# A hybrid encoder layer on one core: the rest of the modulation moved to column quarters of TensorE, with an earlier load of each head's decays and a longer pause in the DeltaNet inverse

## The chip, the core and the metric

The kernel runs on one core of one Trainium2 chip. The metric is the device time of one execution in microseconds (us), the median of several runs. All data is float32; the large products are done as three products of a split into a rounded part and a rest (float32r), so that they keep float32's precision.

The engines are named as in the profile: PE is TensorE (its weight loads are PEld), DVE is VectorE, ACT is ScalarE, POOL is GpSimd, SP is SyncE, whose queue issues nearly all transfers. Each engine, SP's queue too, works through its own instructions in order: one that waits holds up all that stand behind it.

## What is computed

One layer for 512 prompt frames and 64 sample frames, width 2048. A vector `c` for each of the two streams gives six modulation vectors; they scale and shift the input of the mixer and of the feed-forward part, and gate both results.

```python
mod = jax.nn.silu(c) @ w_ada[l] + b_ada[l]
sh1, sc1, g1, sh2, sc2, g2 = jnp.split(mod[:, None, :], N_MOD, axis=-1)
h = rmsnorm(x, norm1[l]) * (1 + sc1) + sh1
mix, s_a, s_b, s_c = token_mixers(h, ...)        # 4 GLA heads and 8 DeltaNet heads
x = x + g1 * mix
h = rmsnorm(x, norm2[l]) * (1 + sc2) + sh2
f, s_f = conv_ffn(h, ...)
x = x + g2 * f
```

`w_ada` is 2048 x 12288. The DeltaNet recurrence of a head needs, for each block of frames, decays `exp(G_i - G_j)`, a triangular inverse and products with it:

```python
decay = jnp.exp(jnp.where(causal, big_g[..., :, None] - big_g[..., None, :], -jnp.inf))
lower = jnp.where(strict, jnp.einsum('bhid,bhjd->bhij', kb, k) * decay, 0.0)
sol = lax.linalg.triangular_solve(eye + lower, rhs, left_side=True, lower=True, unit_diagonal=True)
```

## The kernel before

The program has five stages. The head (0 to 205 us of the profiled span) loads and transposes x, works out the first two modulation vectors (`sh1`, `sc1`) and starts some projections. The mixer (205 to about 1185 us) makes 50 projection tiles of 128 columns (`in_tile`, `gemm`, `mm6`) and beside them runs the recurrences. Two halves of the output projection follow (to 1300 and to 1420 us), then the up products (to 2450) and the down products (to the end).

**What paces the mixer.** A projection tile is 16 steps over the depth of 2048. A step is six matmuls of 288 columns (`mm6`, lines 528 and 530), and after each step `tick` (line 495) is called. A tick advances the recurrences by one step (`job_step`: the oldest job that does not yield `WAIT` does a step, and jobs that yield `WAIT` only count down) and the remaining modulation by 0.65 steps (`ADA_RATE`). `rest(n)` yields `WAIT` n times: it is a pause of n ticks. The order of the instructions on every engine is fixed when the program is built; operations of `self.jv` and `self.ja` (the recurrences' DVE and ACT work) are put some 80 instructions ahead of their place, those of the weight split `L614` to `L616` as well.

**The modulation before.** The vectors three to six are 16 blocks of 512 columns. `ada_block` (line 773) loads two depth steps of a block at a time (512 KB into one of the two `xr` tiles, line 780). DVE multiplies each 128x512 slab by the stream's column of `silu(c)` and adds it to an accumulator: for each block 16 depth steps x 2 streams = 32 DVE operations (lines 786 and 788). The partitions are then summed by 8 matmuls with a column of ones (line 794). In the head the first two vectors are done another way (`modulation`, line 675): four depth steps at once on the four 32-column quarters of PE's array (line 688), each quarter with its own 32 PSUM partitions, then a copy, a transpose and a sum of the four quarters (lines 691 to 694).

**A DeltaNet head.** The job `gdn` (line 163) begins by loading the head's cumulated decays, broadcast over the partitions, into `gb` (line 181). ACT makes the decay matrices `dl` and `du` from it. PE transposes keys and queries and makes `k k^T` (line 224), DVE makes the matrix `a` from it and from `dl`. `inverse16` (line 340) then inverts the 16x16 diagonal blocks: `a` goes to DRAM (`d0`, line 350), comes back as 32 lanes (line 356), POOL does 28 small operations (lines 362 and 363), the result goes to DRAM (`d1`, line 367) and comes back as `cm` (line 371); DVE spreads it into `t` and `u` (line 376), and after a pause of `REST_U` ticks the products of the inverse begin: pairs of matmuls (lines 246 and 252) with a DVE operation after each. POOL's work of all jobs is kept in the order in which it is recorded (`_InTurn`): the power in the output norm of one head stands ahead of the next head's 28 operations.

Tiles of 128x512 come from pools with a fixed number of buffers: 13 under the tag `m` (`gb` is one), 7 under `qkv`.

Of the kernel before, what the change touches and what calls it, by code (L numbers as in the profile page):

```python
# [8 lines left out]
F32 = mybir.dt.float32  # L9
# [3 lines left out]
ALU = mybir.AluOpType  # L13
# [3 lines left out]
P = 128  # L17
D = 2048
KD = 16
# [16 lines left out]
REST_S, REST_L, REST_D, REST_X, REST_U, REST_T, REST_N, REST_O, REST_G = 2, 3, 6, 4, 4, 2, 4, 4, 3  # L36
# [60 lines left out]
class Kern:  # L97
# [65 lines left out]
    def gdn(self, qF, kF, x, gain, hcols, gb_src, s0, s_out, o_put, last_level):  # L163
# [16 lines left out]
        gb = self.m4()  # L180
        nc.sync.dma_start(gb, gb_src.partition_broadcast(P))
# [151 lines left out]
        o_put(kF)  # L333

# [288 lines left out]
    def head(self, pool):  # L623
# [8 lines left out]
        nc.gpsimd.memset(cs, 0.0)  # L632
        for s in range(2):
            A.activation(self.ct[:, s], self.vmap[f"c{s}"], AF.Silu)
            V.tensor_copy(cs[:, :, s], self.ct[:, s])
# [39 lines left out]
        def modulation(g):  # L675
            for mi in (1, 0):
                ps = self.bank()
                c0 = mi * D + g * 512
                for k0 in range(0, KD, 4):
                    yield  # L680
                    raws = [hraw().rearrange("p (k n) -> p k n", k=2) for _ in range(2)]
                    for n, raw in enumerate(raws):
                        k1 = k0 + 2 * n
                        nc.sync.dma_start(raw, i["w_ada"][0, k1 * P:(k1 + 2) * P, c0:c0 + 512].rearrange("(k p) n -> p k n", p=P))

                    for k in (2, 3, 0, 1):
                        with self.tc.issue_after(last) if k == 0 else nullcontext():
                            T.matmul(ps[32 * k:32 * k + 32], cs[:, k0 + k], raws[k // 2][:, k % 2], start=(k0 == 0), stop=(k0 == KD - 4))  # L688
                        last = nc.cur_bb.bb.instructions[-1]
                rw = pool.tile([P, 512], F32, tag="rw", bufs=1, name=self.name("rw"))  # L690
                V.tensor_copy(rw, ps)
                pc = self.transpose4(rw.rearrange("p (b t) -> p b t", b=4))
                m = pool.tile([P, 4, 2], F32, tag="msum", bufs=2, name=self.name("msum"))
                V.tensor_reduce(m, pc.rearrange("p b (j q) -> p b q j", j=4)[:, :, 0:2], axis=mybir.AxisListType.X, op=ALU.add)
                self.put_mod(mi, 4 * g, m)
                for _ in vectors:
                    pass
            self.scale_mod(s1, 1, "norm1", 4 * g)
# [8 lines left out]
        for g in range(4):  # L707
# [23 lines left out]
            for _ in mods:  # L731
                pass

# [39 lines left out]
    def ada_block(self, blk, acc, raw):  # L773

        nc = self.nc
        V, T = nc.vector, nc.tensor
        acc = [a() for a in acc]
        for k0 in range(0, KD, 2):
            w = raw().rearrange("p (k n) -> p k n", k=2)
            nc.sync.dma_start(w, self.i["w_ada"][0, k0 * P:(k0 + 2) * P, blk * 512:(blk + 1) * 512]  # L780
                              .rearrange("(k p) n -> p k n", p=P))
            for k in range(2):
                for s in range(2):
                    col = self.ct[:, s, k0 + k:k0 + k + 1]
                    if k0 + k == 0:
                        V.tensor_scalar_mul(acc[s], w[:, k], col)
                    else:
                        V.scalar_tensor_tensor(acc[s], w[:, k], col, acc[s], op0=ALU.mult, op1=ALU.add)  # L788
                    yield
        yield from self.rest(4)  # L790
        pc = self.bank()
        for j in range(4):
            for s in range(2):
                T.matmul(pc[:, 2 * j + s:2 * j + s + 1], acc[s][:, j * P:(j + 1) * P], self.c["ones"][:, 0:1],
                         start=True, stop=True)
        self.put_mod(blk // 4, 4 * (blk % 4), pc[:, :8].rearrange("p (j s) -> p j s", s=2))

    def ada_blocks(self, blocks, acc):
        for blk in blocks:
            yield from self.ada_block(blk, acc, self.xr)  # L800
# [154 lines left out]
    def gdn_heads(self):  # L955
# [9 lines left out]
        def qk(h):  # L965
            q = conv_tile(0, OFF_BQ, h)
            if h == 0:
                self.narrow(self.kp)
            k, x = conv_tile(1, OFF_BK, h), {}
            self.jobs.append(self.gdn(q, k, x, self.vec("gdn_norm", 0), slice(4 * h, 4 * h + 4),  # L970
                                      self.gd[4 * h:4 * h + 4], None, o["p_gdn"][0, 0, h],
                                      lambda t: self.put_o(8 + h, t), 64))
            return x
# [27 lines left out]
    def gdn_samples(self):  # L1001
        for _ in self.gdn(self.get_s("q"), self.get_s("k"), dict(v=lambda: self.get_s("v"), gate=lambda: self.get_s("g")),
                          self.vec("gdn_norm", 0), slice(32, 36), self.gd[32:36], _States(self, "state_gdn", P),
# [549 lines left out]
def layer_kernel(tc, i, o):  # L1553
    nc = tc.nc
    with ExitStack() as ctx:
# [16 lines left out]
        with ExitStack() as early:  # L1572
            K.wp = pool(early, "wp", "right", bufs=3)
            with ExitStack() as right:
# [9 lines left out]
                with ExitStack() as st:  # L1584
# [3 lines left out]
                    acc = [lambda n=n: K.ap.tile([P, 512], F32, tag=f"acc{n}", bufs=1, name=K.name("acc")) for n in range(2)]  # L1588
# [87 lines left out]
class _MixPool:  # L1676

    BUFS = {"m": 13, "qkv": 7, "gt": 3}
# [42 lines left out]
```

## Time and profile before

| | us |
|---|---|
| median of three runs | 3003.5 |
| the three runs | 3003.4, 3003.5, 3010.31 |
| the profiled execution, its own time | 3013.53 |
| its span, first to last instruction | 3011.7 |
| PE busy in the span | 2885.0 (96%) |
| DVE busy in the span | 2055.7 (68%) |
| mean granted clock of PE | 0.973 |

The span is what the profile shows; 1.8 us of the execution lie outside it. The profiled execution is 10 us longer than the two shorter runs. A row of the windows view gives, for a stretch of the span, how long each engine was busy in it, with the count of instructions, then the granted clock of PE as a share of full speed, the busy share of the DMA engines and GB/s. A row of the waits view gives who waited (engine, tile, line), what ended the wait, the sum in us, the number of times and the longest. A row of the timeline gives start and length in us, the engine, the line, the operation and the tiles; in brackets behind it is idle time of the engine just before, with what ended it. Rows of the same instruction are merged there, "x8" being eight records: a float32 matmul leaves two.

### The profile page before, as it was taken

Reading aid. Unit: us, or ns where it says so; the run is one execution under the profiler, and the core shown is the slowest. Engines: PE = TensorE matmul, PEld = TensorE weight load, DVE = VectorE, ACT = ScalarE, POOL = GpSimd, SP = SyncE. Lnnn points to the kernel's source line nnn. Section 1 sums busy time; section 2 is a strip of 40 time slices with the busy share of each in tenths; the row PEclk is TensorE's granted clock in tenths of the full one; section 3 lists DMA queues with packets and bytes.
Section 4 is the critical chain, followed back from the end, with each engine's and each line's share of the span. In section 5 each row is a group of like instructions: output and inputs, shape, how many; then the busy total and the mean of one; then the engine's idle time right before and its main releaser. Section 6 shows DMA issues by size and latency. Waiting matters only on the chain.

```text
span 3011.7 us, 52193 instructions
## 1 busy us (share of the span) xinstructions
PE 2885.0 (96%) x21060; PEld 2788.5 (93%) x21060; DVE 2055.7 (68%) x3283; ACT 1185.1 (39%) x2019; POOL 286.6 (10%) x513
## 2 busy tenths in 40 slices
PE   6999999988999999999999999999999999999998
PEld 3689888888999899899999999999999999999998
DVE  2367766655668777657888888888888865555555
ACT  4235444433444533245444444444444431222223
POOL 0002211222220000000001101100110100000000
PEclk7999999998999999999999999999999999999999
DMA  7865544434454454843333343333333373333221
GB/s 249 284 191 147 144 126 128 128 115 116 132 159 135 119 168 128 239 135 111 93 114 104 103 114 103 103 114 103 103 114 104 117 248 100 113 101 108 89 85 65
DMA packets 535445, 395.55 MB, mean 131 GB/s; under 512 B 59657, under 2 KB 465412, under 8 KB 535204
## 3 DMA queue, kind: packets, MB, share of 16 engines
q1 hardware_dynamic: 527860, 390.54, 43.5%
q8 instruction: 166, 2.72, 0.4%
q10 hardware_dynamic: 7344, 1.67, 0.3%
q14 instruction: 75, 0.61, 0.1%
HBM read 356.47 MB, written 35.67 MB: 130 GB/s over the span
## 4 chain that ended last, share of the span: by engine, by line
PE 74%; issue 9%; DVE 6%; POOL 5%; DMA 4%; ACT 2%; SPq 1%; ACTq 0%; POOLq 0%; DVEq 0%
PE g L528 23%; PE bank L1320 11%; PE g L530 11%; PE bank L1319 11%; PE bank L1321 11%; POOL m L1657 4%; DVE acc L788 2%; PE bank L688 1%; DMA xr<-in_w_ada_dram 1%; PE bank L152 1%; PE bank L419 1%; DMA m<-gd 1%; ACT m L1642 1%; PE bank L252 1%; DMA xr<-in_x_prompt_dram 1%
## 5 line engine op out<-in xcount | busy, mean ns | idle before, releaser
L1320 PE MATMUL bank<-slot,wh 128*128 128x290 f32 x2464 | 737.3, 299 | 0.0
L1319 PE MATMUL bank<-slot,wh 128*128 128x290 f32 x2464 | 733.2, 298 | 0.0
L1321 PE MATMUL bank<-slot,wl 128*128 128x290 f32 x2464 | 728.3, 296 | 0.0
L528 PE MATMUL g<-slot,wh 128*128 128x288 f32 x3168 | 552.7, 295 | 0.3 <-DVE slot L1089 0.2
L528 PE MATMUL g<-hh,wh 128*128 128x288 f32 x2048 | 474.4, 310 | 4.5 <-DVE conv_in L932 2.9
L1321 PEld LDWEIGHTS bank<-slot,wl 128*128 128x128 f32 x2464 | 470.6, 191 | 0.0
L1320 PEld LDWEIGHTS bank<-slot,wh 128*128 128x128 f32 x2464 | 468.7, 190 | 0.1
L528 PEld LDWEIGHTS g<-slot,wh 128*128 128x128 f32 x3168 | 464.5, 188 | 0.9 <-DVE slot L1089 0.5
L1319 PEld LDWEIGHTS bank<-slot,wh 128*128 128x128 f32 x2464 | 463.7, 188 | 0.1
L615 ACT ACTIVATE wh<-raw 128x1024 fp32r<-128x1024 f32 x215 | 227.2, 1058 | 599.5 <-PE g L528 574.1
L530 PE MATMUL g<-hh,wl 128*128 128x288 f32 x2048 | 460.5, 304 | 1.6 <-DVE wl L616 1.6
L528 PE MATMUL g<-hl,wh 128*128 128x288 f32 x2048 | 459.7, 304 | 0.0
L1089 DVE SCALAR_TENSOR_TENSOR slot<-g,mod,slot 128x512 f32<-128x512 f32 (+1 forms) x448 | 202.0, 491 | 282.9 <-PE g L530 281.9
L788 DVE SCALAR_TENSOR_TENSOR acc<-xr,ct,acc 128x512 f32<-128x512 f32 x480 | 341.7, 752 | 44.0 <-DMA xr<-in_w_ada_dram 43.5
L528 PEld LDWEIGHTS g<-hh,wh 128*128 128x128 f32 x2048 | 337.0, 193 | 17.5 <-issue 10.0
L530 PEld LDWEIGHTS g<-hh,wl 128*128 128x128 f32 x2048 | 339.1, 193 | 8.7 <-issue 5.9
L528 PEld LDWEIGHTS g<-hl,wh 128*128 128x128 f32 x2048 | 339.3, 193 | 4.4 <-issue 4.0
L530 PE MATMUL g<-slot,wl 128*128 128x288 f32 x1584 | 342.6, 295 | 0.0
L616 DVE TENSOR_TENSOR wl<-raw,wh 128x1024 fp32r<-128x1024 f32 x215 | 262.0, 1218 | 51.8 <-ACT wh L615 51.2
L1266 ACT ACTIVATE wh<-raw 128x1024 fp32r<-128x1024 f32 x176 | 186.1, 1058 | 223.0 <-PE bank L1320 190.7
L530 PEld LDWEIGHTS g<-slot,wl 128*128 128x128 f32 x1584 | 256.1, 188 | 0.0
L1267 DVE TENSOR_TENSOR wl<-raw,wh 128x1024 fp32r<-128x1024 f32 x176 | 215.2, 1223 | 54.4 <-ACT wh L1266 54.4
(350 smaller groups left out, 3151.5 us busy)
## 6 DMA issues: line engine op xcount, KB each, us to landing
raw<-in_w_up_dram SPq DMA_DIRECT2D x176, 512.0 KB
xr<-in_w_ada_dram SPq DMA_DIRECT2D x128, 512.0 KB
raw<-in_w_in_dram SPq DMA_DIRECT2D x100, 512.0 KB
raw<-in_w_down_dram SPq DMA_DIRECT2D x88, 512.0 KB
hraw<-in_w_ada_dram SPq DMA_DIRECT2D x64, 512.0 KB
raw<-in_w_out_dram SPq DMA_DIRECT2D x32, 512.0 KB
slot<-actd SPq DMA_DIRECT2D x44, 288.0 KB
actd<-v SPq DMA_DIRECT2D x44, 256.0 KB
```

The costliest lines, as they stand in the source:

```text
L528: T.matmul(ps[:, h if bank is None else bank, :n], wh, x[:, h, :n], start=f, stop=False)
L530: T.matmul(ps[:, h if bank is None else bank, :n], wl, ah[:, h, :n], start=False, stop=stop)
L615: nc.scalar.activation(hi[:, :n_], raw[:, :n_], AF.Copy)
L616: nc.vector.tensor_tensor(lo[:, :n_], raw[:, :n_], hi[:, :n_].bitcast(F32), op=ALU.subtract)
L788: V.scalar_tensor_tensor(acc[s], w[:, k], col, acc[s], op0=ALU.mult, op1=ALU.add)
L1089: self.nc.vector.scalar_tensor_tensor(x1[:, :, z], ps[:, :, c], gain[:, q:q + 1], x1[:, :, z], op0=ALU.mult, op1=ALU.add)
L1266: self.nc.scalar.activation(hi, src, AF.Copy)
L1267: self.nc.vector.tensor_tensor(lo, src, hi.bitcast(F32), op=ALU.subtract)
L1319: T.matmul(ps, wh[:, j], hi, start=(c < 3 and j == 0), stop=False, skip_group_check=True)
L1320: T.matmul(ps, wh[:, j], lo, start=False, stop=False, skip_group_check=True)
L1321: T.matmul(ps, wl[:, j], hi, start=False, stop=(j == NPAIR - 1), skip_group_check=True)
L1657: r = f(*a, **kw)
```

## The change

The remaining 16 blocks of the modulation are done as those in the head: `ada_block` loads four depth steps into both `xr` tiles (two transfers of 512 KB), pauses six steps, does the four products on PE's quarters (`quad`, 128x32 by 128x512 each) into a PSUM bank, and DVE copies or adds that bank into one accumulator of 128x512. After four such rounds the accumulator is transposed, and the quarters are summed as in the head (`quad_sum`). A column matrix `c_col` of 128x16x32 is kept for the mixer. The pause of steps between rounds makes 8 yields in a round, 32 in a block; before it was 36 in a block.

`decays` loads `gb` ahead of the projection tile of the head's keys; before, the job's first step did. `REST_U` goes from 4 to 8. The tag `m` has 12 buffers, `qkv` 8. The head's own modulation runs the same steps through the shared functions.

```diff
-REST_S, REST_L, REST_D, REST_X, REST_U, REST_T, REST_N, REST_O, REST_G = 2, 3, 6, 4, 4, 2, 4, 4, 3
+REST_S, REST_L, REST_D, REST_X, REST_U, REST_T, REST_N, REST_O, REST_G = 2, 3, 6, 4, 8, 2, 4, 4, 3
...
-        gb = self.m4()
-        nc.sync.dma_start(gb, gb_src.partition_broadcast(P))
...
+    def decays(self, rows):
+
+        gb = self.m4()
+        self.nc.sync.dma_start(gb, self.gd[rows].partition_broadcast(P))
+        return gb
...
-    def ada_block(self, blk, acc, raw):
-
-        nc = self.nc
-        V, T = nc.vector, nc.tensor
-        acc = [a() for a in acc]
-        for k0 in range(0, KD, 2):
-            w = raw().rearrange("p (k n) -> p k n", k=2)
-            nc.sync.dma_start(w, self.i["w_ada"][0, k0 * P:(k0 + 2) * P, blk * 512:(blk + 1) * 512]
-                              .rearrange("(k p) n -> p k n", p=P))
-            for k in range(2):
-                for s in range(2):
-                    col = self.ct[:, s, k0 + k:k0 + k + 1]
-                    if k0 + k == 0:
-                        V.tensor_scalar_mul(acc[s], w[:, k], col)
-                    else:
-                        V.scalar_tensor_tensor(acc[s], w[:, k], col, acc[s], op0=ALU.mult, op1=ALU.add)
-                    yield
-        yield from self.rest(4)
-        pc = self.bank()
-        for j in range(4):
-            for s in range(2):
-                T.matmul(pc[:, 2 * j + s:2 * j + s + 1], acc[s][:, j * P:(j + 1) * P], self.c["ones"][:, 0:1],
-                         start=True, stop=True)
-        self.put_mod(blk // 4, 4 * (blk % 4), pc[:, :8].rearrange("p (j s) -> p j s", s=2))
+    def quad(self, ps, c, raws, start, stop):
+
+        for k in (2, 3, 0, 1):
+            with self.tc.issue_after(last) if k == 0 else nullcontext():
+                self.nc.tensor.matmul(ps[32 * k:32 * k + 32], c[:, k], raws[k // 2][:, k % 2], start=start, stop=stop)
+            last = self.nc.cur_bb.bb.instructions[-1]
+
+    def load_ada(self, raws, blk, k0):
+        raws = [r.rearrange("p (k n) -> p k n", k=2) for r in raws]
+        for n, r in enumerate(raws):
+            k1 = k0 + 2 * n
+            self.nc.sync.dma_start(r, self.i["w_ada"][0, k1 * P:(k1 + 2) * P, blk * 512:(blk + 1) * 512].rearrange("(k p) n -> p k n", p=P))
+        return raws
+
+    def quad_sum(self, rw, m):
+
+        pc = self.transpose4(rw.rearrange("p (b t) -> p b t", b=4))
+        self.nc.vector.tensor_reduce(m, pc.rearrange("p b (j q) -> p b q j", j=4)[:, :, 0:2], axis=mybir.AxisListType.X, op=ALU.add)
+
+    def ada_block(self, blk, acc):
+
+        V = self.nc.vector
+        acc = acc()
+        for k0 in range(0, KD, 4):
+            raws = self.load_ada([self.xr(), self.xr()], blk, k0)
+            yield from self.rest(6)
+            ps = self.bank()
+            self.quad(ps, self.c_col[:, k0:k0 + 4], raws, True, True)
+            if k0 == 0:
+                V.tensor_copy(acc, ps)
+            else:
+                V.tensor_tensor(acc, ps, acc, op=ALU.add)
+            yield from self.rest(2)
+        m = self.sp.tile([P, 4, 2], F32, tag="msum", bufs=2, name=self.name("msum"))
+        self.quad_sum(acc, m)
+        self.put_mod(blk // 4, 4 * (blk % 4), m)
...
+            gb = self.decays(slice(4 * h, 4 * h + 4))
             k, x = conv_tile(1, OFF_BK, h), {}
-            self.jobs.append(self.gdn(q, k, x, self.vec("gdn_norm", 0), slice(4 * h, 4 * h + 4),
-                                      self.gd[4 * h:4 * h + 4], None, o["p_gdn"][0, 0, h],
+            self.jobs.append(self.gdn(q, k, x, self.vec("gdn_norm", 0), slice(4 * h, 4 * h + 4), gb, None, o["p_gdn"][0, 0, h],
                                       lambda t: self.put_o(8 + h, t), 64))
...
-    BUFS = {"m": 13, "qkv": 7, "gt": 3}
+    BUFS = {"m": 12, "qkv": 8, "gt": 3}
```

**On DVE**, where the third DeltaNet head's inverse begins its products: `m_3326` (before) and `m_3205` (now) is the first product's masked result, which PE's second product waits for; `m_3968` and `m_3955` is the inverse `u`. Before:

```order
L788 SCALAR_TENSOR_TENSOR acc_3922<-xr_3978,ct,acc_3922 128x512
L788 SCALAR_TENSOR_TENSOR acc_3921<-xr_4065,ct,acc_3921 128x512
L788 SCALAR_TENSOR_TENSOR acc_3922<-xr_4065,ct,acc_3922 128x512
L788 SCALAR_TENSOR_TENSOR acc_3921<-xr_4065,ct,acc_3921 128x512
L1642 TENSOR_TENSOR m_3326<-bank_4021,consts_1740 128x256
L932 COPY conv_in<-g_3848 128x64
L616 TENSOR_TENSOR wl_4270<-raw_4268,wh_4269 128x1024
L1642 TENSOR_TENSOR m_3968<-m_3968,bank_4034 128x16x16
```

The same place in the changed kernel; `kt_4023` holds the next head's key factors:

```order
L804 TENSOR_TENSOR acc_3729<-bank_3936,acc_3729 128x512
L620 TENSOR_TENSOR wl_4250<-raw_4248,wh_4249 128x1024
L944 COPY conv_in<-g_3842 128x64
L951 COPY cs<-conv_in 128x6
L948 SCALAR_TENSOR_TENSOR ca_3981<-conv_in,cols,ca_3981 128x579 x3
L945 COPY conv_in<-cols 128x3
L1656 TENSOR_TENSOR m_3205<-bank_4093,consts_1740 128x256
L145 TENSOR_SCALAR kt_4023<-s_587_4022 128x4
L620 TENSOR_TENSOR wl_4369<-raw_4367,wh_4368 128x1024
L1656 TENSOR_TENSOR kt_4023<-kt_4023 128x4
L1656 TENSOR_TENSOR m_3955<-m_3955,bank_4105 128x16x16
```

The modulation's operations are gone from ahead of the masked result, and the first factors of the next head now stand between it and the update of `u`.

**On SP's queue**, around the load of the fifth head's decays (`m_4939` before, `m_4642` now, from `gd`); `d_594` and `d_612` are the fourth head's `d1`, which waits for POOL's 28 operations. Before:

```order
L356 DMA m_4468<-d_593_4236 8x16x16 x4
L317 DMA out_dram<-st_4427 128x128
L614 DMA raw_4927<-in_w_in_dram 128x8x128
L945 DMA od_73<-qkv_3173 256x1x256
L367 DMA d_594_4237<-m_4468 32x2x256
L371 DMA cm_4744<-d_594_4237 128x4x16 x2
L614 DMA raw_5077<-in_w_in_dram 128x8x128
L181 DMA m_4939<-gd 128x512
L780 DMA xr_4767<-in_w_ada_dram 128x2x512
```

Now:

```order
L784 DMA xr_4354<-in_w_ada_dram 128x2x512
L360 DMA m_4452<-d_611_4218 8x16x16 x4
L315 DMA out_dram<-st_4415 128x128
L336 DMA m_4642<-gd 128x512
L784 DMA xr_4506<-in_w_ada_dram 128x2x512
L784 DMA xr_4507<-in_w_ada_dram 128x2x512
L618 DMA raw_4952<-in_w_in_dram 128x8x128
L957 DMA od_73<-qkv_3178 256x1x256
L371 DMA d_612_4219<-m_4452 32x2x256
```

The decays' load has moved from behind `d1` and `cm` to ahead of them, and the modulation's loads stand in pairs.

**On PE**, at the same products as on DVE above (`bank_4021` before, `bank_4093` now). Before:

```order
L528 MATMUL g_4008<-hl_551,wh_4010 128x288 x2
L530 MATMUL g_4008<-hh_550,wl_4011 128x288 x2
L246 MATMUL bank_4021<-m_3968,m_3400 128x64 x4
L528 MATMUL g_4008<-hh_562,wh_4010 128x288 x2
L528 MATMUL g_4008<-hl_563,wh_4010 128x288 x2
L530 MATMUL g_4008<-hh_562,wl_4011 128x288 x2
L528 MATMUL g_4008<-hh_581,wh_4010 128x288
L252 MATMUL bank_4034<-m_3326,m_3967 128x64 x4
```

Now, with the next head's keys (`qkv_3980`) and queries (`qkv_3826`):

```order
L152 MATMUL bank_4024<-consts_96,qkv_3980 128x128 x4
L152 MATMUL bank_4056<-consts_96,qkv_3826 128x128 x4
L222 MATMUL bank_4081<-qkv_3980 128x128 x4
L244 MATMUL bank_4093<-m_3955,m_3282 128x64 x4
L534 MATMUL g_3994<-hh_915,wl_3997 128x288
L532 MATMUL g_3994<-hh_1180,wh_4142 128x288 x2
L532 MATMUL g_3994<-hl_1181,wh_4142 128x288 x2
L250 MATMUL bank_4105<-m_3205,m_3954 128x64 x4
```

The next head's transposes and its product of the keys, which came later before, now stand directly ahead of the inverse's first product.

More of the change, by code (lines that the diff above doesn't have):

```diff
@@ L161, in col4, with gdn @@
         return cols.unsqueeze(2).to_broadcast([P, cols.shape[1], w])
-    def gdn(self, qF, kF, x, gain, hcols, gb_src, s0, s_out, o_put, last_level):
+    def gdn(self, qF, kF, x, gain, hcols, gb, s0, s_out, o_put, last_level):
         nc, c = self.nc, self.c
@@ L631, in head @@
         cs = pool.tile([P, KD, 32], F32, tag="cs", bufs=1, name="cs")
-        nc.gpsimd.memset(cs, 0.0)
         for s in range(2):
             A.activation(self.ct[:, s], self.vmap[f"c{s}"], AF.Silu)
-            V.tensor_copy(cs[:, :, s], self.ct[:, s])
+        self.c_columns(cs)
         self.mod = self.cp.tile([P, 6, KD, 2], F32, name="mod")
@@ L677, in modulation @@
                 ps = self.bank()
-                c0 = mi * D + g * 512
                 for k0 in range(0, KD, 4):
                     yield
[L681 to L689, printed above, removed]
+                    raws = self.load_ada([hraw(), hraw()], mi * 4 + g, k0)
+                    self.quad(ps, cs[:, k0:k0 + 4], raws, k0 == 0, k0 == KD - 4)
                 rw = pool.tile([P, 512], F32, tag="rw", bufs=1, name=self.name("rw"))
                 V.tensor_copy(rw, ps)
-                pc = self.transpose4(rw.rearrange("p (b t) -> p b t", b=4))
                 m = pool.tile([P, 4, 2], F32, tag="msum", bufs=2, name=self.name("msum"))
-                V.tensor_reduce(m, pc.rearrange("p b (j q) -> p b q j", j=4)[:, :, 0:2], axis=mybir.AxisListType.X, op=ALU.add)
+                self.quad_sum(rw, m)
                 self.put_mod(mi, 4 * g, m)
@@ L732, in head, with c_columns @@
                 pass
+    def c_columns(self, cs):
+        self.nc.gpsimd.memset(cs, 0.0)
+        for s in range(2):
+            self.nc.vector.tensor_copy(cs[:, :, s], self.ct[:, s])
     def pair_w(self, offs, k0):
@@ L798, in ada_blocks @@
     def ada_blocks(self, blocks, acc):
         for blk in blocks:
-            yield from self.ada_block(blk, acc, self.xr)
+            yield from self.ada_block(blk, acc)
     def w_in(self, off):
@@ L1002, in gdn_samples @@
         for _ in self.gdn(self.get_s("q"), self.get_s("k"), dict(v=lambda: self.get_s("v"), gate=lambda: self.get_s("g")),
-                          self.vec("gdn_norm", 0), slice(32, 36), self.gd[32:36], _States(self, "state_gdn", P),
+                          self.vec("gdn_norm", 0), slice(32, 36), self.decays(slice(32, 36)), _States(self, "state_gdn", P),
                           self.o["s_gdn"][0, 0],
@@ L1587, in layer_kernel @@
                     K.dp = dp
-                    acc = [lambda n=n: K.ap.tile([P, 512], F32, tag=f"acc{n}", bufs=1, name=K.name("acc")) for n in range(2)]
+                    acc = lambda: K.ap.tile([P, 512], F32, tag="acc", bufs=1, name=K.name("acc"))
+                    K.c_col = K.ap.tile([P, KD, 32], F32, name="c_col")
+                    K.c_columns(K.c_col)
                     K.ada = K.ada_blocks(range(8, 24), acc)
```

## Prediction

> **What bounds the kernel now.** I read the busy shares first, then windows by stage, then PE's waits in the stage where it idles, then the timeline around such waits.
>
> ```profile
> PE 2885.0 (96%) x21060; PEld 2788.5 (93%) x21060; DVE 2055.7 (68%) x3283; ACT 1185.1 (39%) x2019; POOL 286.6 (10%) x513
> ```
>
> ```profile
> 205.00:880.00 675.00, 615.45 (x4448) 593.52 (x4447) 439.91 (x803) 309.70 (x766) 150.73 (x309) 0.94 0.47 135
> 880.00:1185.00 305.00, 293.34 (x2124) 278.21 (x2123) 234.56 (x466) 125.72 (x236) 12.85 (x17) 0.98 0.45 131
> 1185.00:1300.00 115.00, 109.12 (x774) 104.06 (x772) 69.34 (x103) 31.65 (x52) 1.65 (x16) 0.97 0.76 213
> 1420.00:2450.00 1030.00, 1027.19 (x7610) 1026.32 (x7610) 855.39 (x1076) 465.95 (x569) 108.99 (x137) 1.00 0.40 116
> ```
>
> A row gives the stretch, the busy time of PE, PEld, DVE, ACT and POOL, then the granted clock. PE is the bound. In the up products it idles 2.8 of 1030 us at full clock, so nothing is to be had there. From 205 to 1300 us it idles 59.6 + 11.7 + 5.9 = 77 us, and 0.06 x 675 + 0.02 x 305 + 0.03 x 115 = 50 us of full clock are missing. Only these two sums can pay for PE work that is added; DVE, 439.9 of 675 us busy, counts only where PE waits for it. PE's waits there, who waited, what ended it, sum, times, longest:
>
> ```profile
> PE bank L252 <- DVE conv_in L932: 14.2, 3, 5.2
> PE bank L252 <- DVE m L1642: 14.2, 3, 6.6
> PE bank L246 <- DVE m L376: 12.5, 5, 4.1
> PE bank L152 <- ACT m L1642: 6.7, 8, 1.5
> PE bank L419 <- DVE m L1642: 5.2, 2, 4.4
> PE bank L152 <- DMA xr<-in_x_prompt_dram: 4.3, 6, 2.1
> PE bank L152 <- ACT qkv L940: 3.9, 4, 1.6
> PE bank L246 <- DVE sq L998: 3.4, 1, 3.4
> PE g L528 <- DVE conv_in L932: 2.9, 2, 2.6
> ```
>
> More than half stands at the inverse's products (L246, L252). The timeline around one shows how it arises:
>
> ```profile
> 395.29 1.28 ACT L1642 ACTIVATE m<-m,ncum 128x128 f32<-128x128 f32 x4 [7.08 <-DMA m<-gd]
> 397.27 2.54 DVE L936 SCALAR_TENSOR_TENSOR ca<-conv_in,cols,ca 128x579 f32<-128x579 f32 x3 [3.59 <-ACT ca L934]
> 404.57 4.16 DVE L788 SCALAR_TENSOR_TENSOR acc<-xr,ct,acc 128x512 f32<-128x512 f32 x5
> 408.65 0.41 DVE L1642 TENSOR_TENSOR m<-bank,consts 128x256 f32<-128x256 f32 x1
> 409.21 1.94 PE L252 MATMUL bank<-m,m 128*128 128x64 f32 x8 [5.15 <-DVE conv_in L932]
> ```
>
> ACT stands 7.08 us for the next head's decays; the convolution on DVE comes 3.59 us late for that, the accumulations pile up behind it, and the masked result that PE needs is written only at 409. After the wait the clock is down:
>
> ```profile
> 409.20:415.20 6.00, 5.99 (x30) 5.98 (x30) 3.01 (x5) 1.16 (x2) 0.00 (x0) 0.55 0.49 128
> 415.20:420.00 4.80, 4.80 (x43) 4.57 (x43) 4.22 (x8) 0.94 (x2) 0.00 (x0) 1.00 0.21 76
> ```
>
> 30 records took 6.0 us at 0.55; at the next row's rate they take 30 x 4.8 / 43 = 3.35. A long wait costs 2.65 us more than its own length.
>
> **Added on PE: the quads.** 16 blocks x 4 rounds = 64. The head's quad, among the same products:
>
> ```profile
> 77.48 0.43 PE L530 MATMUL g<-hh,wl 128*128 128x288 f32 x2
> 77.84 0.16 PEld L688 LDWEIGHTS bank<-hraw,cs 128*32 128x32 f32 x8 [0.17 <-issue]
> 77.84 1.06 PE L688 MATMUL bank<-hraw,cs 128*32 128x512 f32 x8
> 78.83 0.53 PE L528 MATMUL g<-hh,wh 128*128 128x288 f32 x2
> ```
>
> From the start of L530's pair to the start of L528's pair are 1.35 us. Without a quad a matmul follows the one before it after 0.27 (120.00 to 120.27, below), so a quad costs 1.08: **+69 us**. It lies in the way of PE's other work whole, since PE is the bound; I keep 64 to 75 for it.
>
> The Trainium skill ("TensorE: Matmul & The Clock Gate", Part 3, "Packing small matmuls — row/col tiling") says that weight loads overlap running matmuls only where the row group differs; column quarters share all rows. By it the four products would come one behind the other: my estimate is four times the 1.06 of the row, less what the row has, +3.2 a quad. The row speaks against it: eight loads within 0.16 us and all eight records within 1.06.
>
> **Removed on PE: the column sums; added: transposes.** 16 runs of eight L794 go, four transposes a block come:
>
> ```profile
> 392.84 0.42 PE L530 MATMUL g<-hh,wl 128*128 128x288 f32 x2
> 393.10 1.84 PE L794 MATMUL bank<-consts,acc 128*128 128x1 f32 x16
> 394.80 0.51 PE L528 MATMUL g<-hh,wh 128*128 128x288 f32 x2
> ```
>
> ```profile
> 119.03 0.60 PE L152 MATMUL bank<-consts,rw 128*128 128x128 f32 x4
> 119.38 0.52 PE L528 MATMUL g<-hl,wh 128*128 128x288 f32 x2
> ...
> 120.00 0.43 PE L528 MATMUL g<-hh,wh 128*128 128x288 f32 x2
> 120.27 0.43 PE L528 MATMUL g<-hl,wh 128*128 128x288 f32 x2
> ```
>
> 16 x (1.96 - 0.27) = **-27**; 16 x 0.35 = **+6**. PE's own work thus grows by 48 us, and that is sure to some 5 us.
>
> **DVE** loses its accumulations and gets 64 copies or adds:
>
> ```profile
> L788 DVE SCALAR_TENSOR_TENSOR acc<-xr,ct,acc 128x512 f32<-128x512 f32 x480 | 341.7, 752 | 44.0 <-DMA xr<-in_w_ada_dram 43.5
> L1642 DVE TENSOR_TENSOR m<-bank,m 128x512 f32<-128x512 f32 x18 | 12.0, 684 | 5.1 <-ACT m L1642 3.0 <-POOL m L1657 2.0
> ```
>
> 342 us go, 64 x 0.684 = 44 come: some 300 us less. That is worth nothing by itself; it is worth the waits below. The accumulations' own waits for loads (43.5 us) go from DVE's order as well: no L788 can hold up a masked result any more.
>
> **The waits at the inverse.** The decays' load passes `d1` and `cm` of the head before on SP's queue, of which `d1` waits for POOL; it lands while the key tile's 96 matmuls run, and ACT's 7.08 us stall goes, with what it delays. If that cover were gone, the stall and the lateness of the convolution stay as they are. `REST_U` 8 gives the spread of `cm` four more ticks, each longer than six matmuls at 0.27, so 6.5 us or more against a longest L246 wait of 4.1. L252 (14.2 + 14.2), L246 (12.5 + 3.4) and L528 (2.9) make 47.2 us; the bounds are 0 and -47. I take **-40**: the first causes are all touched, the rest stays since DVE still has the splits of the weights and the convolution in its order.
>
> **The clock.** These rows count 14 waits; I take ten as long enough for the 2.65 us: **-27**. The bounds are 0 and -50, the whole missing clock. Not all of it follows waits:
>
> ```profile
> 441.90:445.30 3.40, 3.40 (x17) 3.40 (x17) 1.40 (x4) 1.41 (x6) 0.00 (x0) 0.50 0.92 235
> 687.70:691.10 3.40, 3.40 (x16) 3.40 (x16) 1.81 (x5) 0.28 (x1) 0.00 (x0) 0.50 0.00 0
> ```
>
> Both stretches are at half clock with PE busy throughout, and just ahead of the first stands only the longest of the L940 waits, 1.6 us. So a short wait can cost clock as well, half of 3.4 = 1.7 us, and I count that in the upper bound below. The same page of the Trainium skill (Part 1, on the clock gate) ties half speed to an idle window of about 3.4 us, by which short new waits would cost no clock; this row speaks against it.
>
> **The other waits.** The modulation now has 64 x 8 yields, at 0.65 a tick 788 ticks, where 576 yields took 886; its transfers no longer lie beside the x tiles that the output projection fetches (L152, 4.3). L419 (5.2) waits for DVE, L152 for ACT (6.7 + 3.9). Of these 20 us I take **-9**, bounds 0 and -20.
>
> **New waits at the products.** With the longer pause they stand behind the next head's transposes and its product of the keys on PE, and behind its key factors on DVE, which wait for ACT's squares. Queued behind a late masked result are PE's second product and with it the projection. The nearest rows are L152's waits for ACT, 6.7 / 8 = 0.8 and 3.9 / 4 = 1.0 us, and L246's longest, 4.1. Seven heads have a next head: 7 x 1.1 = **+8**, bounds 0 and 7 x (4.1 + 1.7) = 41. I take the short rows, as the transposes wait in the same way.
>
> **New waits of the quads.** A quad needs both loads of its round; before, DVE took a load as it came and PE did not care. Both `xr` tiles are rewritten in each round, so a load is issued only after the quad before. What stands in front on SP's queue:
>
> ```profile
> SPq L367 <- POOL m L1657: 96.6, 9, 14.6
> 534.13 12.98 POOL L1657 TENSOR_TENSOR m<-m 32x14 f32<-32x14 f32 x28
> 552.51 4.82 DMA xr<-in_w_ada_dram
> ```
>
> A round has 8 yields = 12.3 ticks; between two loads and their quad lie 6 yields, 9.2 ticks of over 1.6 us, 15 us. A landing of 4.8 fits three times; behind a `d1` that holds the queue up to 14.6 us it does not. Eight heads hold it up once each, and most loads are not then due: one us a head, **+8**; bounds 0 and 50 (eight heads at 14.6 + 4.8 - 15 = 4.4 us, with the clock's 2.65 after each, 56, of which nearly all).
>
> **Sum:** 69 - 27 + 6 - 40 - 27 - 9 + 8 + 8 = **-12 us**. The profiled execution took 3013.5, so its like would take 3001.5. It stands 10 us above the median of the runs, which I take as the base, since two of three runs agree: 3003.5 - 12 = **2991.5**, say 2991.
>
> **The rivals.** *All of the waits go* (B): no new ones worth more than 3 us, the L528, L246 and L252 rows empty, 40 us of clock back: 48 - 47 - 40 - 9 + 3 = -45, 2958. For it: DVE is freed of 300 us. Against: the key factors in front of the masked result.
>
> *The waits come back at the new place* (C): the order on DVE puts key factors that wait for ACT, and ACT for POOL's power of the head before, in front of the masked result of L244's product. If that lateness passes about 3 us a head, what is saved is spent: with 40% of the waits and of their clock gone, and 11 of new ones at quads and transposes, 48 - 16 - 11 - 4 + 11 = +28, 3031. For it speaks that PE's order there now has three producers in a row; against it that ACT loses its 7 us stall.
>
> *The pairs come late* (D): a quad that stands on PE for a load stops the projection too. At the upper bound, -12 - 8 + 50 = +30, 3033. It decides from some 2 us a head, with the clock. The waits of L367 (96.6 us) speak for it, the pause of 15 us against it.
>
> *The early load isn't early* (E): `m` has 12 tiles in place of 13, and the load waits on SP's queue for a free one, ahead of `d1`. ACT's stall and L252's 28 us stay, only L246 gains: 48 - 16 - 10 + 8 for the quads = +30, 3033.
>
> *Quads one after another* (F): 64 x 3.2 = +205 over the forecast, 3196, by the overlap rule named above.
>
> **How the numbers follow.** A has 0.46, B 0.18, C 0.18, D 0.11, E 0.06, F 0.01. A's own range is 2975 to 3003. Some 9 us, 0.3%, is about what a measurement of this kernel can tell from no change. Faster by more (below 2994.5): B, and 0.33 of A, and nothing of C to F: 0.51. Slower by more (above 3012.5): C, D and E less a few hundredths that end milder, with F: 0.27. The rest, 0.22, is the upper end of A and those mild endings. The range, 2950 to 3036, takes B's time and C, D and E's; outside are F, the steeper half of D, and a B that gains the last of the clock.
>
> **What would show it.** Right: waits of PE for DVE at L250 and L244 below 10 us together, ACT's wait for `m<-gd` near 0, the clock in 205 to 880 at 0.97 or more, DVE 300 us less busy, 64 quads (L777) with starts of the neighbours 1.35 apart. C: waits at L250, L244 and L222 for DVE or ACT above 25 us. D: waits of L777 for `xr` above 20. E: ACT's wait for `m<-gd` still above 20, with SP standing at L336. F: eight records of L777 over 4 us. The forecast is wrong in its base, not in a mechanism, if PE's busy time at full clock grows by anything but 48.

## The result, and the profile after

The changed kernel takes 2989.8 us (median of five runs, 2981.4 to 2993.2) where the kernel before takes 3003.5: a ratio of 0.9942, with a 95% interval of 0.9921 to 0.9962. In a later series it took 2989.3 against 3008.9, ratio 0.9931 (0.9918 to 0.9943). The prediction was 2991, range 2950 to 3036. Its profiled execution is the fastest of the five, 2981.4, with a span of 2979.7.

The page's shares, and the windows of the same four stretches:

```profile
PE 2898.3 (97%) x21380; PEld 2742.7 (92%) x21380; DVE 1778.4 (60%) x2853; ACT 1180.8 (40%) x2017; POOL 267.5 (9%) x514
```

```profile
205.00:880.00 675.00, 651.89 (x4860) 584.10 (x4859) 278.32 (x544) 313.79 (x780) 136.17 (x315) 0.98 0.49 147
880.00:1185.00 305.00, 296.24 (x2154) 263.70 (x2153) 156.72 (x339) 123.68 (x230) 8.92 (x26) 0.99 0.46 139
1185.00:1300.00 115.00, 115.00 (x847) 111.72 (x846) 40.40 (x57) 31.33 (x55) 0.02 (x1) 1.00 0.58 159
1420.00:2450.00 1030.00, 1030.00 (x7658) 1030.00 (x7657) 845.69 (x1051) 455.78 (x542) 106.76 (x131) 1.00 0.40 118
```

From 205 to 1300 PE now idles 23.1 + 8.8 + 0 = 31.9 us in place of 77.1, and 0.02 x 675 + 0.01 x 305 = 16.6 us of full clock are missing in place of 50. PE's waits there:

```profile
PE bank L777 <- DMA xr<-in_w_ada_dram: 7.1, 5, 3.3
PE bank L152 <- DVE acc L804: 6.1, 2, 5.9
PE bank L459 <- ACT junk L1656: 3.1, 1, 3.1
PE bank L486 <- DVE m L1656: 2.5, 5, 0.8
PE bank L777 <- issue: 2.0, 1, 2.0
PE bank L152 <- DMA xr<-in_x_prompt_dram: 1.6, 2, 1.3
PE bank L250 <- DVE m L1656: 1.6, 1, 1.6
...
PE bank L244 <- DVE rq L145: 0.9, 1, 0.9
```

The rows at the inverse's products (now L244 and L250) have shrunk from 44.6 us to 2.8; the quads (L777) and the transposes of the accumulator (L152 for `acc`) have brought waits of their own, 15 us. ACT's wait for the decays, before and now:

```profile
ACT m L1642 <- DMA m<-gd: 33.2, 6, 13.0
```

```profile
ACT m L1656 <- DMA m<-gd: 3.7, 2, 3.3
```

A quad on PE's timeline:

```profile
304.98 0.44 PE L534 MATMUL g<-hh,wl 128*128 128x288 f32 x2
305.35 1.06 PE L777 MATMUL bank<-xr,c_col 128*32 128x512 f32 x8
306.35 0.52 PE L532 MATMUL g<-hh,wh 128*128 128x288 f32 x2
```

Start to start 1.37 us, so 1.10 more than the 0.27 without it.

A balance that the experiments use throughout: span, less PE's idle time from 205 to 1300, less the missing full clock there, leaves what PE has to do. Before it is 3011.7 - 77.1 - 50.0 = 2884.6, now 2979.7 - 31.9 - 16.6 = 2931.2. The windows' clock has two digits, and kernels with the same work of PE differ by up to 9 us in it, so a single figure is good to some 5 us. (Idle time at half clock is counted twice, which lowers the rest a little where there is much of both.)

### The profile page after: what moved, and what is told of

It is laid out like the page before. It is cut to its first block, busy times and chain, and to the rows that moved or that the text cites. A ratio compares the mean times of both kernels' runs of the same rounds, so it can differ in the third digit from the quotient of the medians.

```text
span 2979.7 us, 52428 instructions
## 1 busy us (share of the span) xinstructions
PE 2898.3 (97%) x21380; PEld 2742.7 (92%) x21380; DVE 1778.4 (60%) x2853; ACT 1180.8 (40%) x2017; POOL 267.5 (9%) x514
## 4 chain that ended last, share of the span: by engine, by line
PE 84%; issue 5%; DVE 3%; POOL 3%; DMA 2%; ACT 2%; SPq 0%; ACTq 0%; POOLq 0%; DVEq 0%
PE g L532 28%; PE g L534 14%; PE bank L1332 11%; PE bank L1331 11%; PE bank L1333 11%; PE bank L777 3%; POOL m L1671 2%; PE bank L152 1%; PE bank L423 1%; DMA xr<-in_w_ada_dram 1%; DVE ca L948 1%; DVE wl L620 1%; ACT wh L619 0%; PE g L664 0%; PE ps_nar L836 0%
## 5 line engine op out<-in xcount | busy, mean ns | idle before, releaser
L534 PE MATMUL g<-hh,wl 128*128 128x288 f32 x2048 | 454.0, 300 | 0.0
L532 PE MATMUL g<-hl,wh 128*128 128x288 f32 x2048 | 448.7, 299 | 0.0
L532 PEld LDWEIGHTS g<-hh,wh 128*128 128x128 f32 x2048 | 330.2, 190 | 52.0 <-issue 48.9
L532 PEld LDWEIGHTS g<-hl,wh 128*128 128x128 f32 x2048 | 332.8, 190 | 4.5 <-issue 4.2
L1278 ACT ACTIVATE wh<-s 128x1024 fp32r<-128x1024 f32 x132 | 140.2, 1062 | 208.5 <-DVE s L1289 109.2
```

What stands on the lines that cost most here:

```text
L532: T.matmul(ps[:, h if bank is None else bank, :n], wh, x[:, h, :n], start=f, stop=False)
L534: T.matmul(ps[:, h if bank is None else bank, :n], wl, ah[:, h, :n], start=False, stop=stop)
L1278: self.nc.scalar.activation(hi, src, AF.Copy)
```

## The experiments

The change has three parts: the quads (Q), the early load of the decays (E) and the pause of 8 (U8). The question was which of them buys the time. Each kernel was timed against the kernel before on its own chip; the ratios are compared, and "idle" and "clock" are the two sums above, from one profiled execution each. The quads come with 12 buffers under `m` and 8 under `qkv` in each kernel that has them, and the other kernels have 13 and 7; the buffers were not varied by themselves.

| kernel | parts | median us (before) | ratio (95%) | idle | clock | rest |
|---|---|---|---|---|---|---|
| before | none | | 1 | 77.1 | 50.0 | 2884.6 |
| early_alone | E | 3003.8 (3008.9) | 0.9981 (0.9972 to 0.9989) | 71.7 | 43.3 | 2881.6 |
| u8_alone | U8 | 3002.7 (3010.9) | 0.9978 (0.9966 to 0.9990) | 82.4 | 43.3 | 2875.5 |
| order_u6 | E, pause 6 | 2980.4 (3010.9) | 0.9896 (0.9880 to 0.9911) | 58.7 | 40.3 | 2880.0 |
| order_alone | E, U8 | 2979.9 (3010.6) | 0.9902 (0.9885 to 0.9919) | 61.4 | 29.8 | 2882.1 |
| quads_alone | Q | 2996.6 (3010.6) | 0.9959 (0.9945 to 0.9974) | 41.2 | 13.5 | 2939.0 |
| late_decays | Q, U8 | 3003.8 (3010.6) | 0.9978 (0.9968 to 0.9989) | 46.7 | 23.3 | 2934.8 |
| rest_u4 | Q, E | 2980.5 (3010.6) | 0.9912 (0.9895 to 0.9929) | 31.9 | 13.5 | 2932.6 |
| after_again | Q, E, U8 | 2989.3 (3008.9) | 0.9931 (0.9918 to 0.9943) | 34.7 | 16.6 | 2938.5 |
| quads_71 | Q, E, yields 7 and 1 | 2988.2 (3010.9) | 0.9921 (0.9909 to 0.9934) | 36.1 | 9.8 | 2940.2 |
| half_quads | half Q, E | 2996.2 (3008.9) | 0.9959 (0.9947 to 0.9972) | 59.1 | 33.1 | 2900.8 |
| half_quads_u8 | half Q, E, U8 | 2992.9 (3010.9) | 0.9940 (0.9926 to 0.9953) | 58.6 | 25.6 | 2911.3 |
| double_quads | Q twice, E, U8 | 3049.1 (3008.9), one run | | 35.0 | 16.6 | 2995.8 |

**order_alone**: the kernel before with `decays` and the pause.

```diff
-REST_S, REST_L, REST_D, REST_X, REST_U, REST_T, REST_N, REST_O, REST_G = 2, 3, 6, 4, 4, 2, 4, 4, 3
+REST_S, REST_L, REST_D, REST_X, REST_U, REST_T, REST_N, REST_O, REST_G = 2, 3, 6, 4, 8, 2, 4, 4, 3
...
+            gb = self.decays(slice(4 * h, 4 * h + 4))
             k, x = conv_tile(1, OFF_BK, h), {}
```

> The kernel before with the early load of the decays and REST_U 8; the modulation stays on DVE, so PE's work does not grow by 48 us. Theory (waits come half from the decays' load and the short pause, half from DVE's accumulations): L246 and half of L252 empty, 30 us of waits and some 18 us of clock back, less 8 of new waits at the next head's start: about 40 us below before, 2963, which would beat the change. Rival 1 (the order alone causes the waits): 2940 or below, L252 and L246 under 10 us together. Rival 2 (DVE's 340 us of accumulations cause them): within 10 us of before, L250/L252's kind of wait still above 20 us.

Measured: 31 us below before, below the changed kernel too, with DVE as busy as before. The rest is the 2882 of the kernel before; idle time and missing clock fall by 36 together. That is nearest to the theory, whose 40 hoped for a little more. The waits at the products are gone; what is left stands elsewhere:

```profile
PE bank L152 <- ACT qkv L944: 12.7, 4, 6.8
...
PE bank L250 <- DVE m L1647: 1.0, 3, 0.4
PE bank L244 <- DVE m L380: 1.0, 1, 1.0
```

**quads_alone**: the changed kernel with the load of `gb` back in the job and `REST_U` 4.

```diff
-            gb = self.decays(slice(4 * h, 4 * h + 4))
...
+        gb = self.m4()
+        nc.sync.dma_start(gb, gb_src.partition_broadcast(P))
```

> The changed kernel with the decays' load back in the job's first step and REST_U 4. Theory: +48 us of PE work stays, half of the L252 waits and L419's go, the ACT stall for the decays stays: 5 to 25 us slower than before, 3010 to 3028. Rival 1 (order causes the waits): all waits stay, +48 to +60, above 3050. Rival 2 (DVE causes them): within 10 us of the changed kernel, 2980 to 3000.

Measured: 14 us below before, within what rival 2 gave, where the theory had it slower. The quads by themselves nearly empty the rows at the inverse, with ACT standing even longer for the decays than before:

```profile
PE bank L252 <- DVE conv_in L946: 4.8, 2, 2.8
PE bank L246 <- DVE rq L145: 4.3, 1, 4.3
```

```profile
ACT m L1657 <- DMA m<-gd: 49.2, 7, 13.6
```

So ACT's stall by itself does not make the waits at the products: this speaks against the chain that the prediction drew.

**late_decays**: only the load back in the job. **rest_u4**: only the pause back at 4, in the changed kernel.

> The changed kernel with only the decays' load back in the job's first step. Theory: ACT waits again some 30 us for the load, the convolution comes late, DVE has room to catch up, so PE loses 10 to 20 us: 3000 to 3010. Rival 1 (the early load carries the gain): +40 or more, above 3025. Rival 2 (DVE's freedom alone): no change, within 6 us of the changed kernel.

> The changed kernel with only REST_U back to 4. Theory: L244's waits for the spread of cm come back, up to 16 us with some 10 us of clock: 3000 to 3015. Rival (with the decays early and DVE free the spread is in time after 4 ticks): within 6 us of the changed kernel.

Measured: the late load costs 11 to 14 us (0.9978 against 0.9931 and 0.9942), as the theory had it. The short pause costs nothing: 2980.5, ratio 0.9912, at least as fast as the changed kernel; the rival holds. Also without the early load the short pause is the faster (quads_alone against late_decays, 7 us on one chip). With the quads, the pause is no gain; whether it costs a few us the intervals, which overlap, do not settle.

**early_alone** and **u8_alone**: the two parts of order_alone, each by itself. **after_again** is the changed kernel as it is, beside early_alone.

> The changed kernel, unchanged, beside the others on one chip. 15 to 25 us below before, as in its first runs (ratio 0.992 to 0.996) or a little better.

> The kernel before with only the early load of the decays; REST_U 4, modulation on DVE. Theory (the load's place alone carries the gain, the pause nothing): within 8 us of the run with both (2980), about 30 us below before, PE's waits 60 to 65 us from 205 to 1300. Rival (early load and pause are needed together): the waits at L246 for the spread stay, 12 us and their clock, and it lies at most 15 below before.

> The kernel before with only REST_U 8; the decays are loaded in the job's first step, the modulation is on DVE. Theory (the pause moves the products out of the stretch of DVE in which convolution and accumulations are piled up, and the early load matters little): at least 20 us below before, PE's waits in 205 to 1300 some 64 us with L246 and L252 under 10. Rival (pause and early load are needed together, since the products now stand beside the next head's start, which waits for its decays): within 8 us of before, with the waits at the products still above 20.

Measured: early_alone 5 us below before, u8_alone 8, both together 31. For both kernels the rival was right in the time: each part needs the other. (In u8_alone the rival's sign, waits at the products above 20 us, did not come; the loss stands elsewhere.) The waits say why. With the early load alone, ACT no longer stands for the decays at all (its waits have no such row), and yet PE waits at the products for 39.2 us, against 44.6 before:

```profile
PE bank L250 <- DVE conv_in L936: 16.5, 4, 4.9
PE bank L244 <- DVE m L380: 11.5, 5, 3.8
PE bank L250 <- DVE m L1647: 7.7, 2, 5.2
...
PE bank L244 <- DVE sq L1003: 3.5, 1, 3.5
```

DVE's timeline ahead of one of them, in the same kernel, shows what makes the masked result late:

```profile
382.67 1.29 DVE L380 TENSOR_TENSOR m<-cm,consts 128x512 f32<-128x512 f32 x2 [10.74 <-DMA cm<-d]
383.88 1.22 DVE L620 TENSOR_TENSOR wl<-raw,wh 128x1024 fp32r<-128x1024 f32 x1
...
386.08 2.54 DVE L940 SCALAR_TENSOR_TENSOR ca<-conv_in,cols,ca 128x579 f32<-128x579 f32 x3 [0.64 <-ACT ca L938]
...
389.59 2.73 DVE L792 SCALAR_TENSOR_TENSOR acc<-xr,ct,acc 128x512 f32<-128x512 f32 x4
392.25 1.22 DVE L620 TENSOR_TENSOR wl<-raw,wh 128x1024 fp32r<-128x1024 f32 x1
393.38 4.16 DVE L792 SCALAR_TENSOR_TENSOR acc<-xr,ct,acc 128x512 f32<-128x512 f32 x5
397.46 0.41 DVE L1647 TENSOR_TENSOR m<-bank,consts 128x256 f32<-128x256 f32 x1
```

DVE itself stands 10.74 us for `cm` (the inverse of the diagonal blocks, back from POOL by way of DRAM), and what has gathered behind takes it from 382.67 to 397.46, with one gap of 0.64 in it, to work off. Only then comes the masked result. With the pause of 4 PE asks for it at 393.3 (the L250 wait there is 4.72 us).

With the pause alone those waits are gone, and another has come:

```profile
PE bank L152 <- ACT qkv L940: 41.6, 6, 9.2
...
PE bank L252 <- DVE m L1642: 1.3, 3, 0.4
```

```profile
322.63 0.99 ACT L1642 ACTIVATE m<-m,ncum 128x128 f32<-128x128 f32 x3 [13.01 <-DMA m<-gd]
...
334.24 0.63 ACT L940 ACTIVATE qkv<-ca 128x512 f32<-128x512 f32 x1 [1.83 <-DVE ca L936]
...
334.93 1.11 PE L152 MATMUL bank<-consts,qkv 128*128 128x128 f32 x4 [9.09 <-ACT qkv L940]
```

ACT stands 13.01 us for the decays, its part of the convolution and the silu of the next head's keys (`qkv`) come late, and PE stands at the transposes of that tile. So the late load does cost, but only where the products no longer stop PE earlier.

**order_u6**: order_alone with `REST_U` 6.

> The kernel before with the early load and REST_U 6, between the two runs that lie at about -6 (4) and -30 (8) of before. Theory (a matter of place: the products must move out of the stretch of DVE where the convolution stands): L244's waits for cm's spread mostly gone, L250's for DVE still above 12, 8 to 18 below before. Rival (only the spread's lateness, at most 4.1 us, is what the pause pays): two ticks are 3.2 us, so nearly all of it, 22 to 30 below before.

Measured: 2980.4, 31 us below before. Two more ticks do what four do, so the rival was right in the time. The mechanism is nearer to the theory's, a matter of place, though the waits of over 12 us at L250 that it kept did not stay (1.0). A tick is six matmuls, and a row "x2" of the projection on the timeline holds two of them, so a tick is three rows of 0.27 us, some 0.8 us, and not the 1.6 that the expectation counts. With everything else that PE does between, a step took 1.24 us from 205 to 880 in the kernel before (675 us, 1089 records of `hh` with `wh` at L528, two a step). Two ticks are thus 1.6 to 2.5 us, and yet PE's first product of the third head stands 12.7 us later than in early_alone:

```profile
391.32 1.00 PE L244 MATMUL bank<-m,m 128*128 128x64 f32 x8
```

In order_u6:

```profile
381.24 1.30 DVE L380 TENSOR_TENSOR m<-cm,consts 128x512 f32<-128x512 f32 x2 [12.67 <-DMA cm<-d]
...
404.06 1.81 PE L244 MATMUL bank<-m,m 128*128 128x64 f32 x8
...
405.90 0.42 DVE L1647 TENSOR_TENSOR m<-bank,consts 128x256 f32<-128x256 f32 x1 [0.47 <-PE bank L244]
```

DVE stands for `cm` and has its backlog here too, but it is worked off before PE asks: now the masked result waits for PE. The distance in the traces from the start of the spread of `cm` on DVE to PE's first product, is 1 to 12 us in the kernel before and in early_alone (second head to the samples' head), 10 to 24 in order_u6 and 20 to 25 in the changed kernel. Why two ticks move the products so far stays open.

**half_quads** and **half_quads_u8**: every second block on the quarters, the others on DVE by the routine of before; early load; `REST_U` 4 and 8.

```diff
+QUADS = range(0, 16, 2)
...
-            yield from self.ada_block(blk, acc)
+            if (blk - 8) in QUADS:
+                yield from self.ada_block(blk, acc[0])
+            else:
+                yield from self.ada_block_dve(blk, acc)
```

> Early decays, REST_U 4, and only every second block of the modulation on PE's quarters, the others on DVE as before. PE's work grows by 25 us instead of 50. Theory (DVE's backlog makes most of the waits that are left with the early load, and half the relief removes more than half of them): 8 to 15 us below both the early load alone and the changed kernel, some 2968. Rival (relief and price go in step): the same as both, within 5 us.

> Early decays, REST_U 8, every second block of the modulation on PE's quarters, the others on DVE. PE's work +25 over the kernel before. Theory (with the pause DVE's backlog has little effect left, so quads are a price): no better than the early load with the pause on DVE, 2980 to 2988. Rival (half the relief takes more than half of the waits left): 2970 or below.

Measured: 2996.2 and 2992.9. PE's work lies between, as it must (2901 and 2911), but the idle time is 59 in both. With the pause of 4 it was 72 without quads (early_alone) and is 32 with all (rest_u4), so half of the quads remove a third of what all remove; with the pause of 8 it was 61 without (order_alone) and is 32 to 35 with all, so they remove a tenth. Half the relief does not remove half of the waits. The theory of half_quads falls, and its rival too, since the time lies some 7 us from both kernels that it names. The theory of half_quads_u8, that the quads are only a price there, holds in its sense, though the time is higher still by some 5 us: that mixture is as slow as the changed kernel and slower than order_alone.

**double_quads**: the four products of each round twice into one bank.

```diff
-            self.quad(ps, self.c_col[:, k0:k0 + 4], raws, True, True)
+            self.quad(ps, self.c_col[:, k0:k0 + 4], raws, True, False)
+            self.quad(ps, self.c_col[:, k0:k0 + 4], raws, False, True)
```

> The changed kernel with the four products of each round issued twice into the same bank, so that the vectors three to six come out doubled: the price of 64 quads by itself. Theory (1.06 to 1.08 us a quad, in the way of all else): PE's time without waits and slow clock +68, the whole +55 to +70 over the changed kernel. Rival (products on different quarters hide under other matmuls): below +40. Rival (quarters of columns go one after another when issued behind each other): above +130.

Measured, beside after_again's profiled execution: 3049.1 - 2991.6 = 57.5 us; by the balance 2995.8 - 2938.5 = 57. That is 0.9 us for each further quad, from one execution of each: nothing hides it, and nothing lines up one behind the other. The time lies in the theory's range, PE's share below its 68. The vectors three to six come out doubled in this kernel.

**quads_71**: `REST_U` 4, and the yields of a round split 7 and 1.

```diff
-            yield from self.rest(6)
+            yield from self.rest(7)
...
-            yield from self.rest(2)
+            yield from self.rest(1)
```

> The changed kernel with REST_U 4 and the eight yields of a round split 7 before the quad and 1 behind instead of 6 and 2, so that its two loads have one step more. Theory (the quads' waits of 7 to 15 us are loads that come one step too late): L777's waits for xr under 4 us, 8 to 12 us below REST_U 4 alone, 2970 and so below all the others. Rival (they come from the queue of transfers being held up, by more than a step): L777's wait stays above 8 us, no change.

Measured: the time did not fall, nor did the quads' waits, 14.9 us in rest_u4:

```profile
PE bank L777 <- DMA xr<-in_w_ada_dram: 18.3, 9, 4.5
```

The rival holds, and SP's timeline shows what holds the queue up ahead of one of these quads; the quad that waits for these `xr` loads starts at 551.2 after a wait of 1.1 us:

```profile
532.47 0.37 SPq L618 DMA_DIRECT2D raw<-in_w_in_dram  x1
533.16 0.53 SPq L957 DMA_DIRECT2D od<-qkv  x1
541.27 0.34 SPq L371 DMA_DIRECT2D d<-m  x1
542.92 0.92 SPq L375 DMA_DIRECT2D cm<-d  x2
544.26 0.37 SPq L618 DMA_DIRECT2D raw<-in_w_in_dram  x1
544.74 1.75 SPq L784 DMA_DIRECT2D xr<-in_w_ada_dram  x2
```

From 533.7 to 541.3 SP stands at `d1`, which waits for POOL, with the loads behind it; a step more ahead of the quad does not move them past it. The queue is held up by the quads as well: from 205 to 880 SP stands 95.1 us in 32 waits at the `xr` loads, whose tiles the quad before still reads, and 89.4 in 9 for POOL. Which of the two makes most of the 18.3 us stays open.

## Why the prediction came out as it did

**PE's own work** was right. +48 was forecast; the balance has +47 for this pair (2931.2 against 2884.6). It scatters: 2875.5 to 2884.6 for the five kernels with the old modulation, 2931.2 to 2940.2 for the five with one set of all quads (after_again included), and the means lie 55 apart. Summed over the whole span from the clock's records, with the half clock counted only while PE is busy, the same kernels lie within 4 us of each other, and the means 52 apart. A quad costs 1.10 on the timeline (1.08 forecast). The rule of the Trainium skill from which the prediction worked out 4.2 us (page "TensorE: Matmul & The Clock Gate", Part 3, on row and column tiling: weight loads overlap running matmuls only where the row group differs) does not hold here: the eight weight loads of the head's quad took 0.16 us beside its first products, and all eight records 1.06. That the products would run one behind the other was the prediction's own step from that rule; a second quad right behind the first took 0.9.

**DVE** lost 277 us (2055.7 to 1778.4); 300 were forecast.

**The idle time** fell by 45 where -40 - 9 + 8 + 8 = -33 was forecast, **the clock** gave back 33 where 27 was forecast. Both terms were too small, by some 18 us together, against the profiled execution: it fell by 32 (3013.5 to 2981.4), not by 12. Not all of that is the change's: in the head, from 0 to 205, the granted clock was 0.90 in the one profile and 0.94 in the other, which is 8 us of full clock. Against the medians the change is worth 14 in the first series and 20 in the later one. The choice of 3003.5 as base was no better than the profiled 3013.5: the kernel before had medians of 3008.9 to 3010.9 in the three later series. That 2991 lies so near to 2989.8 is in part luck: a low base and a saving put too small met. The signs that the prediction named for its mechanism came: 2.8 us of waits at L250 and L244, 3.7 of ACT's for the decays, a clock of 0.98 from 205 to 880, and 1.37 us between the neighbours of a quad. They show that the waits went, not what had caused them.

**The step that failed is the cause of the waits at L252.** The prediction held that ACT's stall for the decays makes the convolution late, this the accumulations, and these the masked result; "the first causes are all touched". early_alone takes ACT's stall away and keeps 39 of the 45 us, and 4.72 of the 5.15 at the very wait that the prediction showed. A row of the kernel before, just ahead of the timeline that the prediction shows, is not among its rows:

```profile
390.92 1.29 DVE L376 TENSOR_TENSOR m<-cm,consts 128x512 f32<-128x512 f32 x2 [8.33 <-DMA cm<-d]
```

The masked result is late because DVE comes late to it: it stands for `cm` and then has a backlog. That the stall for `cm` is part of the cause is read from the timelines; no run brings `cm` earlier, and DVE stands 38 to 60 us for it in the kernels without these waits too. Two things cure the lateness, each without the other: a pause that is longer by two ticks (order_u6), if the decays are early, which puts the products behind the backlog; and the quads, which take the accumulations out of it (quads_alone). With the quads the products also stand farther behind the spread of `cm`, 10 to 19 us in quads_alone with the old pause; the runs do not separate the two effects. What the prediction priced as one saving of 40 is thus bought twice by the change, and the dearer payment, some 50 us of PE work, is the quads'.

**The length of a tick** was also misread. The prediction takes 0.27 us for one matmul, but that row holds two; a tick is 0.8 us of projection, 1.24 on average, and not 1.6. Four ticks are 3.2 to 5 us and not 6.5, and the six yields ahead of a quad (9.2 ticks) 7 to 11 us and not 15. The products moved by more than the pause's length (order_u6), so this error does not show in the term for the waits.

**The new waits at the products** (rival C) did not come in the change: L244 and L250 wait 2.8 us. A near relative of the mechanism exists: in u8_alone PE waits 41.6 us at the next head's transposes, for ACT's silu. With DVE's accumulations the early load brings that to 12.7 (order_alone); with the quads it is small even with the late load (3.4 in late_decays).

**The pairs that come late** (rival D) came in small: 7.1 us of waits for `xr` and 2.0 for issue against the 8 forecast, and SP's queue standing at `d1`, the place that was named, is seen ahead of one such quad in quads_71.

**The clock's price of a short wait**, of which the prediction had one row, shows again. In the changed kernel PE has one wait over 0.2 us from 780 to 799, at L250, and the half clock stands right behind it:

```profile
795.09 1.13 PE L250 MATMUL bank<-m,m 128*128 128x64 f32 x7 [1.59 <-DVE m L1656]
```

```profile
795.70:799.20 3.50, 3.50 (x18) 3.48 (x17) 0.42 (x1) 3.49 (x8) 1.48 (x3) 0.51 0.04 9
```

The rule of the Trainium skill (same page, Part 1), by which it takes an idle window of about 3.4 us, does not fit these 1.59. Nor is it the wait alone: the half clock from 311.1, from 693.3 and from 983.5 has no row of the waits view in the 8 us ahead of it. What sets it off stays open.

**The version that beats both** is the kernel before with the early load and a pause of 6 or 8: 0.9896 (0.9880 to 0.9911) and 0.9902 (0.9885 to 0.9919), against 0.9942 (0.9921 to 0.9962) and 0.9931 (0.9918 to 0.9943) of the change; only the pause of 8 and the second of these have intervals that just touch. The quads with the early load and the old pause come near (0.9912, 0.9895 to 0.9929).

## What to carry to other kernels

Work moved to the engine that bounds the kernel was paid in full here (52 us, 48 forecast); ask first whether the waits that it is to remove go by a change of place, which costs nothing. Two parts that each bring little can need each other, where one moves a wait and the other removes what makes PE wait at the new place; so parts of a change are tried in pairs as well as singly. And the engine named at the end of a wait may be late from a wait of its own: follow it back on its own timeline, past its nearest wait, before naming the cause.

## What had not been expected

A second quad right behind the first costs 0.9 us (57 / 64), the first 1.10. That the difference, some 0.2, is paid once around a quad and shared by the two is a reading that no run tests.

With the pause of 8, half of the blocks moved to PE left it idle nearly as long as none did: 59 us with half, 61 with none (order_alone), 32 to 35 with all.

Executions of one kernel differ by 0.4%, and by the clock: the changed kernel's five runs have mean clocks of 0.985 to 0.991; the slowest (2993.2) is the one with 0.985, and the two with 0.990 and more are the fastest (2981.4 and 2983.0).
